# Storing expert 0's result whole, and three last stores in place of two, in a batched-experts kernel

## The chip, the cores and the metric

The kernel runs on one core of a Trainium2 chip. Its time is the device time of one execution in microseconds (us); the number compared is the median over several executions. The profile comes from one execution.

## What is computed

Eight experts each push 256 rows of 512 numbers through two layers with a relu between them. Inputs and output are float32.

```
n_experts, capacity, hidden, expert_hidden = 8, 256, 512, 2048
x  : (8, 256, 512)    w1 : (8, 512, 2048)    w2 : (8, 2048, 512)

h = np.matmul(x, w1)
h = np.maximum(h, 0)
return np.matmul(h, w2).astype(np.float32)      # (8, 256, 512)
```

The two weight tensors are 4 MiB per expert and layer in float32, 64 MiB in all; the output is 4 MiB.

## The kernel before

The loop runs over experts. For each expert the whole of w1 and of w2 is loaded to SBUF by GpSimd-issued transfers that turn float32 into bf16 on the way (`load_w1`, L68, and `load_w2`, L72; 2 MiB each on the SBUF side; the w2 of the last two experts comes in two pieces each). Three buffers for each layer's weights are used in turn, so a load is issued when the expert three places before has been used. x is loaded in groups of experts (experts 0 and 1 on SyncE in float32, the others on the gpsimd ring with the cast) and transposed by TensorE (`transpose_x`, L78).

`first_layer(e)` (L103) multiplies with w1 into PSUM, and ScalarE and VectorE evict with relu to `ht_sb` in turn. `second_layer(e)` (L125) multiplies with w2 into two PSUM tiles; then VectorE copies one half of the rows (L138) and ScalarE the other (L139) into `out_sb`, a tile of [128 partitions, 8 experts, 2, 512] float32 that holds the results of all experts until they are stored. On each partition the result of one expert is one run of 4 KB, in SBUF and in DRAM (`out_r`, L40).

The order of the work is written out by hand (a manual schedule, L49): each engine issues its instructions in the order of the code from L145 on. There are two queues of transfers that matter here. GpSimd's ("the gpsimd ring", q0 in the profile) takes its transfers in order: all the weights, and then what L190 and L191 put behind them. SyncE's (q1) takes the loads of x for experts 0 and 1, then the stores of L170 and L194. Both are served by the same 16 DMA engines.

The stores of before are these:

- L170, on SyncE after expert 1's second layer in the code: the last 28 partitions of expert 0's result in five transfers of 12, 4, 4, 4 and 4 partitions (`CUTS`, L32);
- L190, `store(1, 5)` on the gpsimd ring, in the code after the first layers of experts 5 to 7: experts 1 to 4, all partitions;
- L191, on the gpsimd ring: the first 100 partitions of expert 0;
- L194, on SyncE: experts 5, 6 and 7 together, once the last copies to `out_sb` are done.

The kernel ends when every transfer has landed.

Of the kernel before, what the change touches and what calls it, by code (L numbers as in the profile page):

```python
# [10 lines left out]
def kernel(  # L11
# [7 lines left out]
    nc = tc.nc  # L19
# [9 lines left out]
    KT2 = F // P  # L29
    FB = 4  # L30
    WB = 3
    CUTS = (100, 112, 116, 120, 124, 128)  # L32


    GROUPS = ((0, 1), (1, 1), (2, 2), (4, 4))
# [4 lines left out]
    out_r = out.rearrange("e (p mt) n -> p e mt n", p=P)  # L40
# [15 lines left out]
    o_sb = const.tile([P, E, MT, H], f32, name="out_sb")  # L56
# [15 lines left out]
    def load_w2(e):  # L72
        w2_sb[e] = wpool.tile([P, KT2, H], bf, tag="w2", name="w2_sb")
        cuts = {E - 2: (0, 8, 16), E - 1: (0, 9, 16)}.get(e, (0, KT2))
        for lo, hi in zip(cuts, cuts[1:]):
            nc.gpsimd.dma_start(w2_sb[e][:, lo:hi, :], w2_r[e, :, lo:hi, :])  # L76
# [48 lines left out]
    def second_layer(e):  # L125
        po = [
            ps_o.tile([P, H], f32, tag="ps_o", name=f"pt_o{mt}") for mt in range(MT)
        ]
        for kt in range(KT2):
            for mt in range(MT):  # L130
                nc.tensor.matmul(  # L131
                    po[mt][:],
                    ht[e][:, kt, mt * P:(mt + 1) * P],
                    w2_sb[e][:, kt, :],
                    start=(kt == 0),
                    stop=(kt == KT2 - 1),
                )
        nc.vector.tensor_copy(o_sb[:, e, 0, :], po[0][:])  # L138
        nc.scalar.copy(o_sb[:, e, 1, :], po[1][:])  # L139

    def store(e0, e1):
        nc.gpsimd.dma_start(out_r[:, e0:e1], o_sb[:, e0:e1])  # L142
# [23 lines left out]
    load_w1(4)  # L166
    transpose_x(2)
    second_layer(1)
    for p, q in zip(CUTS, CUTS[1:]):
        nc.sync.dma_start(out_r[p:q, 0], o_sb[p:q, 0])  # L170
    load_w2(4)
    first_layer(2, [lambda kt=kt: transpose_x(3, [kt]) for kt in range(KT1)])
    load_w1(5)
# [13 lines left out]
        first_layer(e)  # L187


    store(1, 5)  # L190
    nc.gpsimd.dma_start(out_r[:CUTS[0], 0], o_sb[:CUTS[0], 0])  # L191
    for e in (5, 6, 7):
        second_layer(e)
    nc.sync.dma_start(out_r[:, 5:8], o_sb[:, 5:8])  # L194


# [28 lines left out]
```

## Time and profile before

| | |
|---|---|
| median of 3 executions | 181.9 us (181.53, 181.9 and 455.66) |
| span of the profiled execution, first to last instruction | 180.4 us |
| TensorE busy (matmul) | 126.6 us, 70% of the span |
| VectorE, ScalarE, GpSimd busy | 31.8, 31.6, 12.8 us |
| HBM read and written | 71.30 MB and 4.19 MB, 418 GB/s over the span |
| share of the 16 DMA engines' span in gpsimd-ring packets | 95.4% |

The profiled execution is known by its span alone; its own time was not recorded separately. The median over the executions is 1.5 us above that span.

How to read it: `L12` is line 12 of the kernel. PE is TensorE, DVE VectorE, ACT ScalarE, POOL GpSimd, SP SyncE; a `q` behind the name (POOLq, SPq) is the engine's sequencer, which issues transfers and waits. A row of stretches gives, after the engines' busy times, the granted share of the TensorE clock, the mean busy share of the core's 16 DMA engines (packet records overlap a little, so a full stretch reads 1.01 or 1.02) and the GB/s that they moved. A row of a transfer's landing gives the time from its issue to its last byte.

### The profile page before, as it was taken

Reading aid. Unit: us, or ns where it says so; the run is one execution under the profiler, and the core shown is the slowest. Engines: PE = TensorE matmul, PEld = TensorE weight load, DVE = VectorE, ACT = ScalarE, POOL = GpSimd, SP = SyncE. Lnnn points to the kernel's source line nnn. Section 1 sums busy time; section 2 is a strip of 40 time slices with the busy share of each in tenths; the row PEclk is TensorE's granted clock in tenths of the full one; section 3 lists DMA queues with packets and bytes.
Section 4 is the critical chain, followed back from the end, with each engine's and each line's share of the span. In section 5 each row is a group of like instructions: output and inputs, shape, how many; then the busy total and the mean of one; then the engine's idle time right before and its main releaser. Section 6 shows DMA issues by size and latency. Waiting matters only on the chain.

```text
span 180.4 us, 1831 instructions
## 1 busy us (share of the span) xinstructions
PE 126.6 (70%) x832; PEld 88.8 (49%) x832; DVE 31.8 (18%) x29; ACT 31.6 (18%) x32; POOL 12.8 (7%) x28
## 2 busy tenths in 40 slices
PE   0205989159992199988769594979498967997830
PEld 0104964049840089538733591449388963443300
DVE  0100220102401018610401022012203240101010
ACT  4300240102221026612200030012222220101010
POOL 7300010100101000100100004030010000000000
PEclk9999999957999669999999997899969999999995
DMA  6999999999999999999999999999999999999995
GB/s 244 213 214 200 225 227 209 211 240 202 213 232 225 193 225 225 211 207 229 225 203 211 225 222 203 222 225 207 211 229 225 196 216 207 219 214 212 343 382 230
DMA packets 4286, 40.47 MB, mean 224 GB/s; under 512 B 440, under 2 KB 440, under 8 KB 1976
## 3 DMA queue, kind: packets, MB, share of 16 engines
q0 software_dynamic: 3536, 37.64, 95.4%
q1 hardware_dynamic: 744, 2.74, 3.9%
q8 instruction: 6, 0.10, 0.2%
HBM read 71.30 MB, written 4.19 MB: 418 GB/s over the span
## 4 chain that ended last, share of the span: by engine, by line
DMA 46%; PE 38%; another core or an unknown queue 9%; POOL 2%; issue 1%; ACT 0%; POOLq 0%
DMA w_sb<-in_w_dram 46%; PE pt_o L131 18%; PE pt_h L111 18%; PE pt_tr L88 2%; POOL w_sb L76 1%; POOL w_sb L70 0%; ACT out_sb L139 0%; POOL x_b L66 0%; POOL identity masks.py:199 0%; POOL identity masks.py:197 0%; POOLq masks.py:199 0%; POOLq L209 0%
## 5 line engine op out<-in xcount | busy, mean ns | idle before, releaser
L111 PE MATMUL pt_h<-xt,w_sb 128*128 128x256 bf16 x512 | 65.0, 292 | 31.3 <-DMA w_sb<-in_w_dram 31.3
L111 PEld LDWEIGHTS <-w_sb 128*128 128x128 bf16 x512 | 59.4, 147 | 37.4 <-DMA w_sb<-in_w_dram 34.4
L131 PE MATMUL pt_o<-w_sb,ht_sb 128*128 128x512 bf16 x256 | 58.0, 386 | 9.8 <-DMA w_sb<-in_w_dram 9.8
L131 PEld LDWEIGHTS <-ht_sb 128*128 128x128 bf16 x256 | 25.3, 99 | 41.0 <-issue 11.5
L119 DVE TENSOR_SCALAR ht_sb<-pt_h 128x1024 bf16<-128x1024 f32 x16 | 19.7, 1228 | 65.9 <-PE pt_h L111 65.9
L121 ACT ACTIVATE ht_sb<-pt_h 128x1024 bf16<-128x1024 f32 x16 | 16.5, 1031 | 69.5 <-PE pt_h L111 69.5
L139 ACT COPY out_sb<-pt_o 128x512 f32<-128x512 f32 x8 | 4.7, 586 | 62.9 <-PE pt_o L131 62.9
L138 DVE COPY out_sb<-pt_o 128x512 f32<-128x512 f32 x8 | 5.5, 692 | 57.6 <-PE pt_o L131 57.6
L70 POOL DMA_DIRECT2D w_sb<-in_w_dram x8 | 4.5, 561 | 85.2 <-PE pt_h L111 84.4
L101 DVE COPY xt<-pt_tr 128x1024 bf16<-128x1024 bf16 (+1 forms) x5 | 7.1, 1449 | 17.9 <-PE pt_tr L88 17.9
L88 PE MATMUL pt_tr<-identity,x_b 128*128 128x128 bf16 x64 | 5.3, 234 | 5.1 <-ACT x_b L156 5.1
L99 ACT COPY xt<-pt_tr 128x1024 bf16<-128x1024 bf16 (+1 forms) x5 | 7.4, 1498 | 6.5 <-PE pt_tr L88 3.9
L88 PEld LDWEIGHTS <-x_b 128*128 128x128 bf16 x64 | 4.8, 119 | 5.2 <-ACT x_b L156 5.1
L76 POOL DMA_DIRECT2D w_sb<-in_w_dram x10 | 5.4, 548 | 24.0 <-PE pt_o L131 24.0
L156 ACT ACT_TABLE_LOAD x1 | 1.3, 1283 | 0.7 <-PEq L209 0.7
L156 ACT CAST x_b<-x_f 128x1024 bf16<-128x1024 f32 x1 | 1.0, 1044 | 2.0 <-DMA x_f<-in_x_dram 2.0
L191 POOL DMA_DIRECT2D out_dram<-out_sb x1 | 0.6, 552 | 8.6 <-DMA w_sb<-in_w_dram 8.6
L66 POOL DMA_DIRECT2D x_b<-in_x_dram x2 | 1.1, 552 | 0.0
L157 ACT CAST x_b<-x_f 128x1024 bf16<-128x1024 f32 x1 | 1.0, 1047 | 0.2 <-DMA x_f<-in_x_dram 0.2
L142 POOL DMA_DIRECT2D out_dram<-out_sb x1 | 0.8, 758 | 0.3 <-issue 0.3
masks.py:199 POOL TENSOR_SCALAR_AFFINE_SELECT identity<-identity 128x128 bf16<-128x128 bf16 x1 | 0.3, 289 | 0.1
masks.py:197 POOL MEMSET identity<- 128x128 bf16 x1 | 0.2, 233 | 0.0
(4 smaller groups left out, 0.4 us busy)
## 6 DMA issues: line engine op xcount, KB each, us to landing
w_sb<-in_w_dram POOLq DMA_DIRECT2D x14, 2048.0 KB, 45.8
w_sb<-in_w_dram POOLq DMA_DIRECT2D x2, 1024.0 KB, 46.9
out_dram<-out_sb POOLq DMA_DIRECT2D x1, 2048.0 KB, 53.3
out_dram<-out_sb SPq DMA_DIRECT2D x1, 1536.0 KB, 6.1
w_sb<-in_w_dram POOLq DMA_DIRECT2D x1, 1152.0 KB, 45.0
x_f<-in_x_dram SPq DMA_DIRECT2D x2, 512.0 KB, 3.6
x_b<-in_x_dram POOLq DMA_DIRECT2D x1, 1024.0 KB, 48.4
w_sb<-in_w_dram POOLq DMA_DIRECT2D x1, 896.0 KB, 49.1
```

The lines of the kernel that those rows point to most:

```text
L70: nc.gpsimd.dma_start(w1_sb[e][:], w1_r[e])
L76: nc.gpsimd.dma_start(w2_sb[e][:, lo:hi, :], w2_r[e, :, lo:hi, :])
L88: nc.tensor.transpose(pt[:, i, j, :], x_b[g][:, j, b * KB + i::KT1], identity[:])
L99: nc.scalar.copy(dst, src)
L101: nc.vector.tensor_copy(dst, src)
L111: nc.tensor.matmul(ph[:, i, :], w1_sb[e][:, kt, FB * q + i::KT2], xt[g][:, kt, :, i0:i0 + P], start=(kt == 0), stop=(kt == KT1 - 1),)
L119: nc.vector.tensor_relu(ht[e][:, FB * q:FB * (q + 1), :], ph[:])
L121: nc.scalar.activation(ht[e][:, FB * q:FB * (q + 1), :], ph[:], relu)
L131: nc.tensor.matmul(po[mt][:], ht[e][:, kt, mt * P:(mt + 1) * P], w2_sb[e][:, kt, :], start=(kt == 0), stop=(kt == KT2 - 1),)
L138: nc.vector.tensor_copy(o_sb[:, e, 0, :], po[0][:])
L139: nc.scalar.copy(o_sb[:, e, 1, :], po[1][:])
L156: nc.scalar.copy(x_b[0][:], x_f[:, 0])
```

## The change

The five early stores of expert 0's last 28 partitions go away, and with them the transfer of its first 100 partitions: `store` now takes experts 0 to 4 at once. Experts 5 and 6 get a gpsimd-ring transfer of their own between the second layers of 6 and 7, and SyncE's last store carries expert 7 alone. Nothing else differs.

```
-    CUTS = (100, 112, 116, 120, 124, 128)
...
     second_layer(1)
-    for p, q in zip(CUTS, CUTS[1:]):
-        nc.sync.dma_start(out_r[p:q, 0], o_sb[p:q, 0])
     load_w2(4)
...
-    store(1, 5)
-    nc.gpsimd.dma_start(out_r[:CUTS[0], 0], o_sb[:CUTS[0], 0])
-    for e in (5, 6, 7):
-        second_layer(e)
-    nc.sync.dma_start(out_r[:, 5:8], o_sb[:, 5:8])
+    store(0, 5)
+    second_layer(5)
+    second_layer(6)
+    store(5, 7)
+    second_layer(7)
+    nc.sync.dma_start(out_r[:, 7], o_sb[:, 7])
```

## Prediction

> **What bounds the kernel.** I read the page's DMA row and queues first, then the chain that ended last, then the tail cut into stretches.
>
> ```profile
> DMA  6999999999999999999999999999999999999995
> q0 software_dynamic: 3536, 37.64, 95.4%
> q1 hardware_dynamic: 744, 2.74, 3.9%
> ```
>
> ```profile
> 120.49 49.08 DMA w_sb<-in_w_dram
> 169.57 0.04 issue
> 169.62 3.20 PE pt_o L131 x14
> 172.81 0.02 issue
> 172.84 0.59 ACT out_sb L139
> ```
>
> The DMA engines are at nine tenths from the second slice to the last but one. The chain (start, length, what) ends on the last weight load, landed at 169.57, then 14 matmuls and a copy that ends at 173.43. TensorE only follows the loads. The chain stops there, though the span is 180.4: what follows is stores.
>
> ```profile
> 5.00:120.00 115.00, 82.12 (x544) 57.71 (x544) 22.23 (x20) 21.13 (x22) 6.56 (x14) 0.93 1.01 216
> 120.00:169.60 49.60, 41.32 (x274) 29.85 (x275) 8.92 (x9) 7.61 (x9) 2.34 (x4) 0.97 1.02 219
> 169.60:173.60 4.00, 3.18 (x14) 1.27 (x13) 0.69 (x1) 0.59 (x1) 0.00 (x0) 1.00 1.02 418
> 173.60:173.80 0.20, 0.00 (x0) 0.00 (x0) 0.00 (x0) 0.00 (x0) 0.00 (x0) 1.00 0.67 266
> 174.20:174.40 0.20, 0.00 (x0) 0.00 (x0) 0.00 (x0) 0.00 (x0) 0.00 (x0) 1.00 0.66 266
> 174.40:178.20 3.80, 0.00 (x0) 0.00 (x0) 0.00 (x0) 0.00 (x0) 0.00 (x0) 0.66 1.01 409
> 178.20:178.40 0.20, 0.00 (x0) 0.00 (x0) 0.00 (x0) 0.00 (x0) 0.00 (x0) 0.50 0.58 225
> 178.40:178.60 0.20, 0.00 (x0) 0.00 (x0) 0.00 (x0) 0.00 (x0) 0.00 (x0) 0.50 0.26 102
> 178.60:178.80 0.20, 0.00 (x0) 0.00 (x0) 0.00 (x0) 0.00 (x0) 0.00 (x0) 0.50 0.15 61
> 179.00:179.20 0.20, 0.00 (x0) 0.00 (x0) 0.00 (x0) 0.00 (x0) 0.00 (x0) 0.50 0.06 21
> 179.40:180.40 1.00, 0.00 (x0) 0.00 (x0) 0.00 (x0) 0.00 (x0) 0.00 (x0) 0.50 0.00 0
> ```
>
> The last two columns are the share of the 16 DMA engines and the GB/s. Through loads and stores the share is full (1.01, 1.02) but in two places: from 173.6 to 174.4 a third of the engines stand idle, and from 178.2 they run out one after another, until 0.06, one engine of 16, is left at 179.1. So the end is set by the DMA engine with the most packets to move. The same total has to be moved after the change. Only its spread over engines, and idle time, can change the end.
>
> ```profile
> L142 POOL DMA_DIRECT2D out_dram<-out_sb x1: 758/758/758, 121.4 to 121.4; - x1
> DMA to landing us min/median/max: 53.3/53.3/53.3
> ```
>
> ```profile
> L191 POOL DMA_DIRECT2D out_dram<-out_sb x1: 552/552/552, 130.7 to 130.7; - x1
> DMA to landing us min/median/max: 45.1/45.1/45.1
> ```
>
> ```profile
> L194 SPq DMA_DIRECT2D out_dram<-out_sb x1: 404/404/404, 173.4 to 173.4; - x1
> DMA to landing us min/median/max: 6.1/6.1/6.1
> ```
>
> The gpsimd ring's stores were issued some 50 us early and wait behind weights: experts 1 to 4 land at 121.4 + 53.3 = 174.7, expert 0's 100 partitions at 175.8. SyncE's three experts land at 173.4 + 6.1 = 179.5. About 0.9 us of closing work follows to 180.4.
>
> **The change, part by part.** The sum is made against the span of 180.4; the median of the runs is 1.5 above it, and I carry that difference over.
>
> *Price of a packet.* All stores move in runs of 4 KB.
>
> ```profile
> DMA packets 201, 0.82 MB, mean 412 GB/s; under 512 B 0, under 2 KB 0, under 8 KB 201
> q1 hardware_dynamic: 201, 0.82, 102.0%
> ```
>
> ```profile
> DMA packets 423, 1.66 MB, mean 415 GB/s; under 512 B 18, under 2 KB 18, under 8 KB 423
> q0 software_dynamic: 423, 1.66, 100.9%
> ```
>
> The first is 176 to 178: 2.0 x 16 / 201 = 0.16 us per SyncE packet on an engine. The second is 169.5 to 173.5: 4.0 x 16 / (423 - 18) = 0.16 on the gpsimd ring. Moving a run from one queue to the other costs nothing by these.
>
> *The five early stores go.*
>
> ```profile
> L170 SPq DMA_DIRECT2D out_dram<-out_sb x5: 281/295/384, 33.1 to 34.5; - x5
> ```
>
> ```profile
> DMA packets 296, 3.17 MB, mean 211 GB/s; under 512 B 60, under 2 KB 60, under 8 KB 88
> q1 hardware_dynamic: 56, 0.11, 2.2%
> ```
>
> Five issues of about 0.3, 1.5 us of SyncE; it next has work at 173.4, so nothing. Their data are the second fence (33 to 48): 56 packets, which is 28 of 4 KB and a completion for each. A completion for each row says that a 12-row store ran on 12 engines and each 4-row store on 4. They cost 0.022 x 16 x 15 / 28 = 0.19 us each with the completion.
>
> ```profile
> DMA packets 40, 0.54 MB, mean 212 GB/s; under 512 B 4, under 2 KB 4, under 8 KB 8
> q1 hardware_dynamic: 8, 0.02, 1.9%
> ```
>
> In one turn (39.5 to 42.05) four rows go out, while the gpsimd ring moves 32 packets, two per engine: the four-row stores follow each other turn by turn, as stores on the same four engines would. So I take it that four engines carried five early packets, 5 x 0.19 = 0.95 us, eight more carried one, and four none. As the share stays full up to 173.6, that lag has no idle time to vanish in and reaches the tail. Taken away, the loads of those four engines land up to 0.9 us earlier; on average 28 x 0.19 / 16 = 0.33.
>
> The Trainium skill, DMA: Bandwidth & Descriptors, "Why a DMA increments its semaphore by 16 and not by 1", states that such a store uses the lowest-numbered engines, as many as divide its rows, and that a 100-partition gpsimd copy puts 7 partitions on each of engines 0 to 13, 2 on the next and none on the last. The 28 completions agree; by it engines 0 to 3 hold 12 rows of expert 0 now, 4 to 11 hold 8, 12 and 13 hold 7, then 2 and 0.
>
> *store(1,5) and the 100 partitions become store(0,5).* Expert 0 now puts 128 / 16 = 8 rows on every engine. Before, the 100 late rows are 6.25 on average; the four heavy engines carry at least five early and about six or seven late, so 11 to 12, and lose 3 to 4 packets: 0.16 x 4 = 0.64 us earlier. What they lose, others gain. A gain of one row costs 0.16. The most that an engine can gain is 8 (if it held none), 1.28 us, and such an engine is among those idle between 173.6 and 174.4. GpSimd's issue grows from 0.76 to at most 0.95 (five quarters), at 121.4, with the ring filled for 50 us: nothing.
>
> *store(5,7) comes in on the gpsimd ring.*
>
> ```profile
> 163.66 0.69 DVE L138 COPY out_sb<-pt_o 128x512 f32<-128x512 f32 x1 [6.21 <-PE pt_o L131]
> 163.88 0.59 ACT L139 COPY out_sb<-pt_o 128x512 f32<-128x512 f32 x1 [6.32 <-PE pt_o L131]
> 130.72 0.55 POOL L191 DMA_DIRECT2D out_dram<-out_sb  x1 [8.58 <-DMA w_sb<-in_w_dram]
> ```
>
> It waits for expert 6's copies, which end at 164.47, in place of L191's wait for an earlier load. Behind it GpSimd has nothing but the end of the kernel. Its issue costs between the 0.55 and the 0.76 of the two stores above; I take 0.65, as two experts lie between. By 165.2 its packets stand in a ring that has weights until 169.57 and then 40 packets per engine of store(0,5), 40 x 0.16 = 6.4 us. It is in time by 10 us. If that cover were gone, it would cost its lateness.
>
> *SyncE's last store is a third.* It still waits for the copies at 173.43 and starts as before, but now the ring is not empty then: store(0,5) and store(5,7) are 56 packets per engine, 9.0 us from 169.57 at the latest engine, less at the others. The idle third of 173.6 to 174.4, 0.35 x 0.8 = 0.28 us of all engines, is filled. SyncE's eight packets per engine (1.3 us) share the engines with the ring.
>
> *Sum.* The heavy engines end at 179.2 - 0.64 - up to 0.16 = 178.4 to 178.6. The engines that gain most (8 rows) end at about 178.3, less about 0.8 of idle time filled, plus 1.28: 178.8. One more row on an engine that is already late gives 178.6 to 179.2 + 0.16. I take the last packet at 178.9, 0.3 before the 179.2 of now, for late engines need not all be the heavy ones. Both ends: if all spread vanishes, the idle 0.28 and the 0.82 x 1.0 after 178.2 are won, -1.1 us; if eight rows fall to an engine that is last today, +1.28. Forecast: span 180.1, median 181.9 - 0.3 = 181.6.
>
> **Rivals.** (1) The early stores were a counterweight and the change unbalances the engines: the engine that was spared late rows of expert 0 is one that loses time during the loads, and eight rows more make it last. Against it: the engines run out together at 178.2 but for four (share 0.26 at 178.5), and the spared ones stood idle at 173.6. It decides as soon as such an engine is over 0.9 us late where the loads end. Price: up to 1.28 with nothing saved, 181.9 + 1.2 = 183.1; likelier 0.2 to 0.6. The Trainium skill, DMA: Bandwidth & Descriptors, "Latency and other measured facts", says that engines 7 and 15 are usually slower, which would put engine 15, spared by the rule above, in this place; no row here names engines.
>
> (2) Nothing to be seen: the late engines are not the four heavy ones, but ones with eight rows in both kernels; then 179.2 stays, 181.9.
>
> (3) All spread goes, -1.1: 180.8. For it: the same 0.16 on both queues. Against: load times differ between engines from other causes too, which the change leaves.
>
> (4) store(5,7) comes late or is slow, and the tail waits for it. For over 2%, 3.6 us, it must reach the engines after some 178. Only a long hold of GpSimd's issue would do that, and L142 and L191 show none; 185.5.
>
> **How the numbers follow.** The forecast (0.2 to 0.5 faster) has 0.45, nothing seen 0.2, rival 1 0.25, rival 3 0.07, rival 4 0.03. A measurement of this kernel tells about 2%, 3.6 us, from no change; cases 1 to 3 all lie inside it. So faster 0.02, same 0.94, slower 0.04. The likeliest's own range is 181.2 to 181.8; with the rivals, and with the two plain runs 0.4 apart, 180.8 to 182.6.
>
> **What would show it.** In the profile after: the gpsimd ring's share up, SyncE's data down to 0.5 MB a store and no q1 packets between 33 and 48; the DMA share full from 173.6 to 174.4; engines running out after 178.2 in a shorter tail, the last at about 178.9. Rival 1 shows as a longer tail with one or two engines; rival 4 as a hole in the share after 174. The forecast is wrong if a queue's packets cost more than 0.16 when both queues are served, or if a gpsimd-ring store that lands last ends the kernel later than one of SyncE's does.

## The result, and the profile after

The changed kernel is slower by about half a microsecond. The measurement of 11 runs gave a median of 182.25 us (181.97 to 183.07) against 181.87 for 11 runs of before, ratio 1.0029 with a 95% interval of 1.0015 to 1.0043. The ratio is formed from the fast runs, to which one of before's, of 455.66, does not belong, and it is not the quotient of the two medians. A second measurement beside experiments on one chip (`after_again`, below) gave 1.0038, interval 1.0024 to 1.0052. The median lies within 2% of before and within the forecast range, but on the other side of no change than the forecast of 181.6; only the rivals had made the range that wide, and the likeliest case's own, 181.2 to 181.8, does not hold it.

The profiled execution after took 182.25 us with a span of 180.5. Wherever an execution's own time stands beside its span in these runs, the two are about 1.8 us apart (1.72 to 1.85). By that the profiled execution of before, span 180.4, took about 182.2 (an estimate), which is at the upper end of the plain runs measured beside the changed kernel (181.46 to 182.16). The two spans, 0.1 apart, therefore hide most of the difference, and the tails have to be read by their steps.

The page of the kernel after, the queues:

```profile
DMA  6998999999999899999999998999999999999994
q0 software_dynamic: 3808, 38.80, 96.9%
q1 hardware_dynamic: 432, 1.57, 2.3%
```

As before, the DMA engines are full from end to end. SyncE's queue moves 1.57 MB in place of 2.74, and the gpsimd ring has taken the difference.

The tail after, in stretches (the last two columns are the share of the 16 DMA engines and the GB/s):

```profile
169.00:173.40 4.40, 3.18 (x14) 1.27 (x13) 0.69 (x1) 0.58 (x1) 0.00 (x0) 1.00 1.03 424
173.60:173.80 0.20, 0.00 (x0) 0.00 (x0) 0.00 (x0) 0.00 (x0) 0.00 (x0) 1.00 0.91 369
173.80:174.00 0.20, 0.00 (x0) 0.00 (x0) 0.00 (x0) 0.00 (x0) 0.00 (x0) 1.00 1.00 410
174.40:178.00 3.60, 0.00 (x0) 0.00 (x0) 0.00 (x0) 0.00 (x0) 0.00 (x0) 0.67 0.94 385
178.00:178.20 0.20, 0.00 (x0) 0.00 (x0) 0.00 (x0) 0.00 (x0) 0.00 (x0) 0.50 0.41 164
178.20:178.40 0.20, 0.00 (x0) 0.00 (x0) 0.00 (x0) 0.00 (x0) 0.00 (x0) 0.50 0.35 143
178.40:178.60 0.20, 0.00 (x0) 0.00 (x0) 0.00 (x0) 0.00 (x0) 0.00 (x0) 0.50 0.40 164
178.60:178.80 0.20, 0.00 (x0) 0.00 (x0) 0.00 (x0) 0.00 (x0) 0.00 (x0) 0.50 0.01 0
179.40:180.50 1.10, 0.00 (x0) 0.00 (x0) 0.00 (x0) 0.00 (x0) 0.00 (x0) 0.50 0.00 0
```

The idle third of 173.6 to 174.4 has been filled, as forecast. Some six engines of 16 (0.35 to 0.41) work until 178.6, and then nearly all is done: the last packet ends at 178.74, 0.46 us earlier than in the profiled execution of before (179.20) and near the forecast 178.9. Yet the span ends no earlier. The kernel does not end when every transfer has landed, but when its closing is done, and what comes after the last packet takes longer: 1.7 us after, 1.2 before.

When the stores were issued and landed, from the view of the tile `out_dram` and the list of transfers after:

```profile
L141 POOL DMA_DIRECT2D out_dram<-out_sb x2: 752/820/887, 121.1 to 164.7; - x2
L192 SPq DMA_DIRECT2D out_dram<-out_sb x1: 348/348/348, 173.0 to 173.0; - x1
```

```profile
out_dram<-out_sb POOLq DMA_DIRECT2D x1, 2560.0 KB, 54.2
out_dram<-out_sb POOLq DMA_DIRECT2D x1, 1024.0 KB, 14.1
out_dram<-out_sb SPq DMA_DIRECT2D x1, 512.0 KB, 6.1
```

The ring's last store lands at 164.7 + 14.1 = 178.8, SyncE's at 173.0 + 6.1 = 179.1. Before, the ring was done at 175.8, almost four microseconds ahead of SyncE.

The closing instructions of the two kernels, on the line of the launch. A row gives the shortest, median and longest duration in ns, and the first and last start. The longest is the first: it begins as GpSimd's last store does (164.6 and 164.7 in the kernel after). Before, then after:

```profile
L220 POOLq DRAIN  x3: 40/93/46062, 130.7 to 180.2; - x3
L220 SPq DRAIN  x3: 7/7/7, 179.6 to 179.9; - x3
```

```profile
L218 POOLq DRAIN  x3: 45/102/15062, 164.6 to 180.2; - x3
L218 SPq DRAIN  x3: 7/7/7, 179.2 to 180.0; - x3
```

Before, GpSimd's drain ended at 130.7 + 46.06 = 176.8, almost three microseconds before SyncE had waited for its own store and reached its drain (179.6). After, SyncE is ready at 179.2, but GpSimd's drain lasts until 164.6 + 15.06 = 179.7. In both cases it ends 0.9 to 1.0 us behind the ring's last landing. The engines meet at a barrier at the end of the kernel, so the later of the two counts: GpSimd's first semaphore instruction of the barrier starts at 179.70 before, 0.03 behind the end of SyncE's drains, and at 179.75 after, 0.04 behind the end of its own drain. The waits of SyncE's sequencer show the same (us in total, times, longest), before and then after:

```profile
SPq L220 <- PEq L220: 0.6, 2, 0.5
```

```profile
SPq L218 <- PEq L218: 1.1, 2, 0.7
```

The two waits at the closing barrier last 1.1 us in all in place of 0.6. The engine named (PEq) had long been done, its first closing drain ending at 172.8 before and 172.4 after; the one that comes late is GpSimd.

### The profile page after: what moved, and what is told of

Read it like the earlier page. It is cut to its first block, busy times and chain, and to the rows that moved or that the text cites. A ratio compares the mean times of both kernels' runs of the same rounds, so it can differ in the third digit from the quotient of the medians.

```text
span 180.5 us, 1824 instructions
## 1 busy us (share of the span) xinstructions
PE 127.1 (70%) x832; PEld 89.1 (49%) x832; DVE 31.8 (18%) x29; ACT 31.6 (18%) x32; POOL 13.1 (7%) x28
## 3 DMA queue, kind: packets, MB, share of 16 engines
q1 hardware_dynamic: 432, 1.57, 2.3%
## 4 chain that ended last, share of the span: by engine, by line
DMA 46%; PE 38%; another core or an unknown queue 9%; POOL 2%; issue 1%; ACT 0%; POOLq 0%
DMA w_sb<-in_w_dram 46%; PE pt_o L130 18%; PE pt_h L110 18%; PE pt_tr L87 2%; POOL w_sb L75 1%; POOL w_sb L69 0%; ACT out_sb L138 0%; POOL x_b L65 0%; POOL identity masks.py:199 0%; POOL identity masks.py:197 0%; POOLq masks.py:199 0%; POOLq L207 0%
## 6 DMA issues: line engine op xcount, KB each, us to landing
out_dram<-out_sb POOLq DMA_DIRECT2D x1, 1024.0 KB, 14.1
```

## Experiments

Theory D (the drain): the end is the later of SyncE's last landing and GpSimd's drain, and the drain follows the ring's last landing by some 0.95 us. Theory C (the counterweight, rival 1 of the prediction): the early stores were a counterweight between the DMA engines, and losing it costs the time. The first four kernels ran together on one chip.

### late_only: the late half of the change

```
     (the early stores and the 100 partitions stay)
-    for e in (5, 6, 7):
-        second_layer(e)
-    nc.sync.dma_start(out_r[:, 5:8], o_sb[:, 5:8])
+    second_layer(5)
+    second_layer(6)
+    store(5, 7)
+    second_layer(7)
+    nc.sync.dma_start(out_r[:, 7], o_sb[:, 7])
```

> The late half of the change alone: the early stores and the 100 partitions stay, experts 5 and 6 go on the gpsimd ring, expert 7 on SyncE. Theory D (GpSimd's closing drain ends about 0.94 us after the ring's last transfer has landed, and this now sets the end): the ring lands last at about 178.7 as in the changed kernel, the drain ends near 179.7, the time is 0.3 to 0.5 us above before, ratio 1.0015 to 1.003. Theory C (the early stores were a counterweight between the DMA engines, and their loss is the loss): the counterweight is still there, so ratio 1.000 within 0.001.

Measured: ratio 1.0014, interval 1.0005 to 1.0023. Its drain and its last ring store:

```profile
L222 POOLq DRAIN  x3: 40/93/14681, 164.9 to 180.1; - x3
```

```profile
out_dram<-out_sb POOLq DMA_DIRECT2D x1, 1024.0 KB, 13.7
```

Landed at 164.9 + 13.7 = 178.6, drained at 164.9 + 14.68 = 179.6. The loss is there with the counterweight in place, though a hair below what D expected; the lower end of the interval still lies within the 1.001 that C left open.

### whole0_only: the early half of the change

```
-    store(5, 7)
     second_layer(7)
-    nc.sync.dma_start(out_r[:, 7], o_sb[:, 7])
+    nc.sync.dma_start(out_r[:, 5:8], o_sb[:, 5:8])
```

> The early half alone: experts 0 to 4 in one ring transfer, experts 5 to 7 on SyncE as before. Theory D: the ring lands at about 176.5, GpSimd's drain ends near 177.4, well before SyncE's last landing near 179.1, so the loss is gone: ratio 0.998 to 1.000. Theory C: the whole loss stays, ratio 1.002 to 1.003.

Measured: 1.0006, interval 0.9993 to 1.0020.

```profile
L217 POOLq DRAIN  x3: 40/93/55742, 120.9 to 180.0; - x3
L217 SPq DRAIN  x3: 7/7/7, 179.5 to 179.8; - x3
```

```profile
out_dram<-out_sb POOLq DMA_DIRECT2D x1, 2560.0 KB, 54.8
```

The drain ends at 176.6, 0.9 behind the ring's landing at 175.7 and long before SyncE is ready at 179.5. The median lies a little above what D expected (0.998 to 1.000), and the interval reaches into it. The early half costs nothing that can be told from zero, and it shows no gain either.

### all_ring: expert 7 on the ring too

```
-    nc.sync.dma_start(out_r[:, 7], o_sb[:, 7])
+    store(7, 8)
```

> The changed kernel with expert 7 on the gpsimd ring too, so that SyncE stores nothing. Theory D: the ring now lands last of all, at about 179.1, and the drain ends 0.94 later at about 180.0: 0.3 us over the changed kernel, ratio to before 1.003 to 1.005. Theory C: the bytes per DMA engine are those of the changed kernel, so the same loss as it, 1.002 to 1.003.

Measured: 1.0048, interval 1.0036 to 1.0061.

```profile
L218 POOLq DRAIN  x3: 40/87/6741, 173.3 to 180.5; - x3
```

```profile
out_dram<-out_sb POOLq DMA_DIRECT2D x1, 512.0 KB, 5.7
```

The last store lands at 179.0, no later than SyncE's did in the changed kernel, and the drain ends at 180.0. All engines move the bytes that they move in the changed kernel; only the queue is another.

### split6: expert 6 back on SyncE

```
-    store(5, 7)
+    store(5, 6)
     second_layer(7)
-    nc.sync.dma_start(out_r[:, 7], o_sb[:, 7])
+    nc.sync.dma_start(out_r[:, 6:8], o_sb[:, 6:8])
```

> The changed kernel with expert 6 moved from the ring to SyncE (ring: 0 to 4, then 5; SyncE: 6 and 7). Theory D: the ring has 8 packets per engine fewer, lands 1.2 us earlier at about 177.4, the drain ends near 178.4 and is covered by SyncE's landing near 179.1: ratio 0.998 to 1.000. Theory C: same spread over the engines as the changed kernel, 1.002 to 1.003.

Measured: 1.0009, interval 0.9999 to 1.0018.

```profile
L218 POOLq DRAIN  x3: 45/102/19851, 157.8 to 179.8; - x3
L218 SPq DRAIN  x3: 7/7/7, 179.3 to 179.6; - x3
```

```profile
out_dram<-out_sb POOLq DMA_DIRECT2D x1, 512.0 KB, 18.9
```

The ring lands at 176.7, the drain ends at 177.7 and is covered. The ratio lies above D's expected range (0.998 to 1.000) and below C's (1.002 to 1.003); the interval meets the first alone. Against all_ring, with the same bytes per engine, the intervals are far apart. Against late_only they overlap, so the comparison was repeated further below.

### sync56: experts 5 and 6 on SyncE at the same place

```
-    store(5, 7)
+    nc.sync.dma_start(out_r[:, 5:7], o_sb[:, 5:7])
```

> The changed kernel with the store of experts 5 and 6 moved from the gpsimd ring to SyncE, at the same place in the code. SyncE's 16 packets per engine now go out among the last weight loads, so the ring's own 40 packets of experts 0 to 4 end later. Theory D says that only the ring's last landing counts: I estimate it at 178 to 179, GpSimd's drain 0.95 us behind it at 179 to 180, ratio to before 1.000 to 1.003, and whichever it is, the end of the span lies 0.75 us behind the later of the drain and SyncE's own landing plus 0.13. A theory that a store of its own on the ring costs (its issue, its packets) would give 1.000 or less, with the drain playing no part.

Measured: 1.0027, interval 1.0009 to 1.0044.

```profile
L218 POOLq DRAIN  x3: 45/96/58412, 121.1 to 180.0; - x3
L218 SPq DRAIN  x3: 7/7/7, 179.1 to 179.7; - x3
```

```profile
out_dram<-out_sb POOLq DMA_DIRECT2D x1, 2560.0 KB, 57.5
out_dram<-out_sb SPq DMA_DIRECT2D x1, 1024.0 KB, 9.5
```

This is the telling one. The ring holds experts 0 to 4 alone, as in whole0_only, but SyncE's megabyte goes out ahead of them, so the ring lands at 121.1 + 57.5 = 178.6, drains at 179.5, and the loss is back. By the two ends the drain is some 0.3 us late here, 0.0016, which the wide interval holds. A ring store of its own for experts 5 and 6 is not what costs.

### prefix_probe: which engines are late

The changed kernel, with expert 7 stored by SyncE in nine pieces.

```
-    nc.sync.dma_start(out_r[:, 7], o_sb[:, 7])
+    p = 0
+    for rows in (64, 14, 12, 10, 8, 8, 6, 4, 2):
+        nc.sync.dma_start(out_r[p:p + rows, 7], o_sb[p:p + rows, 7])
+        p += rows
```

> The changed kernel with expert 7's result stored by SyncE in nine transfers of 64, 14, 12, 10, 8, 8, 6, 4 and 2 partitions, to see which DMA engines are the late six: a store of k rows is expected on the k lowest engines, so the number of late landings in each store counts the late engines below k. If the late ones are the six that fetched instructions, as both theories allow, they stand 1.1 us apart from the others in the landings. The time itself is expected at 182 to 183: GpSimd's drain as in the changed kernel, and some 3 us of SyncE issues from 173.

Measured: one run at 182.85, span 181.1. Each of these transfers lands once per DMA engine that it uses. These landings, from the trace (the store of two partitions, issued last at 178.5 and landed at 179.9, is left out):

```
partitions        64     14     12     10     8      8      6      4
engines used      16     14     12     10     8      8      6      4
late landings     6      6      5      3      2      2      1      0
others end by  177.52 177.61 177.68 177.89 178.10 178.31 178.73 178.91
late ones from 178.07 178.28 178.49 178.70 178.90 179.10 179.29   -
```

There are again six late engines, and the counts shrink as the transfers get narrower. No row names an engine. If a narrow transfer uses a subset of the engines of the wider one before it, none of the four that serve four-row stores is late, and if the four are the same in every kernel, they are the ones that carried the early four-row stores of the kernel before.

### The changed kernel, split6 and whole0_only again, on one chip

> The changed kernel once more, on the same chip as the next two. Theory D: GpSimd's drain ends 0.95 us behind the ring's last landing and sets the end, ratio to before 1.0015 to 1.003. If the first measurement of it was a matter of the chip, 1.000.

> Expert 6 on SyncE in place of the ring, beside the changed kernel on one chip. Theory D: drain covered, ratio 0.999 to 1.001, that is 0.2 to 0.5 us under the changed kernel. Theory C (loss of the early counterweight): the same ratio as the changed kernel.

> The early half alone, beside the changed kernel on one chip. Theory D: 0.999 to 1.001. Theory C: the same ratio as the changed kernel. What it differs from 1.000 by is what the early half is worth by itself; the prediction had 0.3 us faster for it, 0.9983.

Measured: after_again 1.0038 (1.0024 to 1.0052), split6_again 1.0005 (0.9989 to 1.0021), whole0_again 1.0011 (0.9997 to 1.0025). The changed kernel's interval lies above the other two but for a hair at whole0_again's upper end, so the loss belongs to the change and not to the chip, and sending expert 6 back to SyncE removes most or all of it. The loss of after_again is above D's range of 1.0015 to 1.003: in its profile the drain makes 0.50 us of the 0.69 that the ratio gives.

All profiles but that of prefix_probe together, in us from the span's start (the ring's and SyncE's last landing, and the drain's end, from the trace):

```
kernel         ring lands  drain ends  behind  SyncE lands  span
before           175.81      176.76     0.95     179.53    180.42
whole0_only      175.70      176.61     0.91     179.43    180.29
whole0_again     175.37      176.28     0.91     179.09    179.97
split6           176.71      177.66     0.95     179.19    180.07
split6_again     176.96      177.91     0.95     179.42    180.29
sync56           178.57      179.48     0.91     179.05    180.22
late_only        178.61      179.60     0.99     179.13    180.37
after            178.76      179.70     0.94     179.09    180.46
after_again      178.90      179.85     0.95     179.22    180.59
all_ring         179.01      180.01     1.00       -       180.74
```

In each row the span is the later of (drain's end) and (SyncE's landing + 0.13), plus 0.73 to 0.77. The first five rows end by SyncE, the last five by the drain. So a ring that lands within some 0.8 us of SyncE's last store, or after it, is what ends the kernel; the 0.8 is an estimate, 0.95 - 0.13, as no row lies between 0.52 us (late_only, ended by the drain) and 2.46 (split6_again, ended by SyncE).

In prefix_probe the ring lands at 178.30 and the drain ends at 179.25, 0.95 behind it as elsewhere. SyncE's last store lands at 179.88 there, and its closing comes some 0.3 us later than in the rows above: SyncE waits for its stores one after another, and five more of these waits, 0.06 us each, stand behind the last landing.

By the same rule the drain ends 0.34 us too late in late_only, 0.48 in after, 0.50 in after_again and 0.30 in sync56; the measured losses are 0.25, 0.53, 0.69 and 0.49, each known to some 0.2 or 0.3.

No version beat the kernel before: whole0_only and split6 equal it within their intervals.

## Why the prediction was wrong

- **What bounds the kernel** held: a full DMA share to the end, and a tail of stores.
- **Packets at 0.16 us on both queues, SyncE's issues at nothing, GpSimd's longer issue at nothing** held: the store of five experts was issued in 0.89 us and the ring stayed full. **store(5,7) in time** held: it was issued at 164.7, in 0.75 us for the 0.65 of the sum, and the share shows no hole. **The idle third filled** held. Most of the signs that the prediction named came out, and the time went the other way.
- **The failed step** is the closing work, which the sum put at no change: "Only its spread over engines, and idle time, can change the end", and "About 0.9 us of closing work follows to 180.4", carried over. It was 0.9 behind SyncE's landing. Behind a landing on the ring it is 0.95 + 0.75 = 1.7. In the profiled execution after, the drain (179.70) ends 0.48 us behind the point (179.09 + 0.13) from which SyncE's landing alone would have closed the kernel; the measured loss is 0.0029 x 181.87 = 0.53. The prediction named "a gpsimd-ring store that lands last ends the kernel later than one of SyncE's does" as something that would make it wrong, but gave it no price and no rival, though the long drain and the landing at 175.8 were both in the trace of before.
- **The heavy engines end 0.64 earlier, and the end 0.3**: this term of the sum was too large, and nothing of it can be told from zero. whole0_only should have been 0.9983 and is 1.0006 and 1.0011. I took the four engines left at the end for the four that carried the early stores. In late_only, which keeps those stores, the load that lands at 47.8 us has four more engines behind than the one before it. By their lags these are among the five that stand 0.75 to 0.92 us behind when the last load lands; the last five stand 1.10 to 1.31 behind. In the kernel after, without any early stores, six engines are 1.1 us late all the same. That is Rival 2's condition, that the late engines are others. In the profile of before itself it is not clear-cut: two of its engines were already 0.9 us behind at 15.7 us, before any store, where no other profile has an engine more than 0.71 behind, so its tail cannot be split cleanly. Together the two terms, 0.3 not won and 0.5 lost, are the distance between the forecast and the measurement.
- **Rival 1** had the direction and not the mechanism: late_only keeps the counterweight and loses, whole0_only drops it and shows no sure loss. A part cannot be excluded: late_only loses less (1.0014) than the whole change (1.0029 and 1.0038), and whole0's 1.0006 and 1.0011 would be 0.1 to 0.2 us, up to 0.45 by the wider interval. **Rival 3** did not occur: the spread stayed, with six engines late. **Rival 4** did not occur.

Where the six late engines come from is argued, not tried. The instruction queue of the kernel after:

```profile
q8 instruction: 6, 0.10, 0.2%
```

In a window around the first of its packets, 28 to 31 us:

```profile
q0 software_dynamic: 38, 0.62, 98.0%
q8 instruction: 1, 0.02, 1.8%
```

One packet of 16 KB takes one engine for 0.018 x 16 x 3 = 0.9 us. The six start at 29.3, 53.6, 77.9, 105.7, 130.0 and 148.7. The weight loads that land at 38, 62, 82, 111, 140 and 154 us have 1, 2, 3, 4, 5 and 6 engines a microsecond behind the rest, and the loads between them have no new one: one more late engine after each packet. The Trainium skill, Runtime: NRT & Kernel Launch, "Instruction fetch mechanics", says that an engine's instructions are refilled in 16 KiB blocks by its own DMA queue and that the cost of crossing such a boundary is mostly hidden. The packets agree in size. By these rows, where the DMA engines are the bound, each packet leaves one of them late to the end of the kernel; no kernel without the packets was run.

## What to carry to other kernels

Two stores that land at the same moment are not worth the same: let the queue whose closing is long finish first. Here that is the gpsimd ring, which by the estimate above has to land some 0.8 us before SyncE's last store to cost nothing, so what is ready last, and enough of it to cover the ring, belongs on SyncE. When a change alters which queue finishes last, price the closing work of that queue, and do not carry over the other one's.

## What the runs showed that I had not expected

GpSimd's closing drain is a long one: 15.06 us after, ending 0.91 to 1.00 us behind the ring's last landing in eleven profiles. The Trainium skill, VectorE: DVE Perf Modes, "The DRAIN you can't avoid", describes the drains ahead of and behind a kernel as constant, some 12 ns, on every engine; SyncE's (7 ns) are about that short, GpSimd's first closing one is not, and neither are those of VectorE (723 ns) and ScalarE (614 ns) in the kernel after. What fills the 0.95 us was not taken apart.

SyncE's last store waits behind a full ring. In the kernel after it is issued at 173.0, and the stretch from 173 to 176 holds no packet of SyncE's queue:

```profile
DMA packets 323, 1.26 MB, mean 419 GB/s; under 512 B 16, under 2 KB 16, under 8 KB 323
q0 software_dynamic: 323, 1.26, 102.0%
```

SyncE's first packet starts at 176.2, more than three microseconds and 323 packets behind the issue. In the kernel before, with some two microseconds of stores left on the ring, SyncE's first packets went out 0.9 us behind the issue; in sync56, where weights were still on the ring, 3.6 us (165.9 to 169.5). By the sum of the packets it should cost nothing here, as all of them have to go anyway; it could cost a small store that something waits for, which was not tried.
